# Later transposes of second-half token blocks, and a larger constant tile, in a fused decoder layer

## The chip, the cores and the metric

The kernel runs on one core of one Trainium2 chip. The metric is the device time of one execution in microseconds, the median of several runs. One launch computes the whole layer.

## The reference, cut to what matters

The layer prepends 16 meta tokens to 1024 tokens of width 1024, mixes them with two groups of heads, projects the mix with `w_out`, adds it to the residual stream and runs a gated feed-forward layer with a short convolution:

```python
h = concatenate([meta, x])                       # 1040 tokens
a = rmsnorm(h, ln_mix_pre)
proj = a @ w_in                                  # 1024 -> 3584
y_diff = diff_attention(dq, dk, dv, ...)         # 4 heads
y_hgrn = hgrn2(hq, hf, hi, hg, ...)              # 4 heads
mix = concatenate([y_diff, y_hgrn]) @ w_out      # 1024 -> 1024
h = h + rmsnorm(mix, ln_mix_post)
a = rmsnorm(h, ln_ffn_pre)
u = causal_conv3(a @ w_ffn_up) + conv_b          # 1024 -> 5632
y = (gelu(u[:, :2816]) * u[:, 2816:]) @ w_ffn_down
h = h + rmsnorm(y, ln_ffn_post)
return h[16:]
```

All inputs and outputs are float32.

## The kernel before, in words

Every large product is made of three products of float32r halves: an operand is split into a rounded part `hi` and a remainder `lo`, and `hi*hi`, `hi*lo` and `lo*hi` are added up in PSUM. The stages run one after the other: input projections together with attention and the recurrent heads; the output projection `w_out` in two column halves; the up-projection of the feed-forward layer, which uses a seven-product scheme on quarters of the matrices (names `pa`, `pb`, `pc`, in `unit`); and the down-projection (names `pd`), made of seven products as well.

**The stage around the change** is the second column half of the output projection (the loop `for i in range(1, NBLK)` that begins with `py = ps_b(f"py1_{i}")`). It runs over eight blocks of 128 tokens. Block i loads its mixed tokens into a tile `mp` (`second_load`, two transfers on the SP queue), and multiplies eight slices of 128 with the split weights, three matmuls of 512 columns each: `run(..., range(4), ...)` is the first twelve matmuls, `run(..., range(4, 8), ...)` the other twelve. Then `post(i, py)` does the norms: ScalarE squares `py` (`junk`), VectorE builds the new residual `xh`, ScalarE squares that, and VectorE writes the normed row block `a2` (printed as `a<-xh,ssy,gfb`). SP stores `xh` to DRAM (`hsc<-xh`).

`trans(i)` turns the normed block: eight 128x128 transposes on TensorE (`pa<-ident,a`, line 1230) into two PSUM banks, and ScalarE copies of them (`at<-pa`) into the tiles `at2` of two token halves: half 0 holds the tokens of blocks 0 to 4 and two of block 5, half 1 the rest. `trans(0)` is the short block of two meta rows. `t_split` and `t_sums` make the operands of the up-projection from `at2` on ScalarE (`t<-at`) and VectorE (`t<-at,t`, `at<-at`). The first up-projection matmuls (`pq`, in `plain_unit`) follow the loop, with `trans(7)` and `trans(8)` between them.

**Order.** TensorE's order is the order of the program (`manual_schedule` for that engine alone). The orders of VectorE, ScalarE, GpSimd and of the SP transfers are set when the kernel is built, by when each instruction is ready there. Each engine and each queue executes in order. Block i's tile `mp` is one of three places, shared in turn:

```python
SLOTS = (("X1", "X2", "mp", "X1", "X2", "mp", "X1", "X2"), ("mp", "X1", "X2", "mp", "X1", "X2", "X1", "mp"))
```

The second row is this stage: block 7 takes the place of block 5, block 6 that of block 3, block 8 that of block 4. Tokens `xh` and the row blocks `a2` have two places each, for odd and even blocks.

**Memory.** `const` tiles are the first on the left side of SBUF. The tiles of the pools opened on the left side follow them: among them the projection inputs `ahi` and `alo`, the blocks `X0`, `X1`, `X2` and `mp`, the split weights of `w_out` (`woh`, `wol`), and most of the up-projection's moving operands `t`. The weights of the projections, of the up-projection (`uh`, `ul`) and all matmul operands of the down-projection (`gh`, `gl`, `wh`, `wl`) are in pools on the right side, as are two of the fourteen operand tiles `t`.

Of the kernel before, what the change touches and what calls it, by code (L numbers as in the profile page):

```python
# [10 lines left out]
F32R = mybir.dt.float32r  # L11
# [6 lines left out]
P = 128  # L18
# [67 lines left out]
def layer_kernel(ctx: ExitStack, tc: tile.TileContext, x, meta, table, lbl, gpre, gpost, win,  # L86
# [25 lines left out]
    def const(shape, name, dt=F32):  # L112
        return cp.tile(shape, dt, tag=name, name=name)
# [12 lines left out]
    nlam = const([P, 1], "nlam")  # L126
    cwt = const([P, 2 * NF, 3], "cwt")
    cbt = const([P, 2 * NF], "cbt")
    m0 = const([P, 46], "m0", F32R)
    G.memset(m0.bitcast(F32), 0.0)  # L130
    m0_7 = const([P, 2, 1, 2], "m0_7", F32R)

# [850 lines left out]
    def load_wo(n):  # L983
        res = []
        for k in range(KD):
            raw = wp.tile([P, 512], F32, tag="wr", name=f"wor{n}_{k}", bufs=3)
            last_load.append(SY.dma_start(raw, wout[P * k: P * (k + 1), 512 * n: 512 * (n + 1)]))
            if n == 0 and k < 2:
                hi = wp.tile([P, 512], F32R, tag="wh", name=f"woh{n}_{k}", bufs=4)
                lo = wp.tile([P, 512], F32R, tag="wl", name=f"wol{n}_{k}", bufs=4)  # L990
            elif k < 5 if n == 0 else k > 5:
                hi, lo = (wsp.tile([P, 512], F32R, tag="wd", name=f"wo{x}{n}_{k}") for x in "hl")
            else:
                hi = wop.tile([P, 512], F32R, tag="woh", name=f"woh{n}_{k}")
                lo = wop.tile([P, 512], F32R, tag="wol", name=f"wol{n}_{k}")
            if n == 0:
                split(hi, lo, raw, V if k else G)
            else:
                with tc.issue_after(ends["a"].ins), tc.issue_after(ends["v"].ins):
                    split(hi, lo, raw, V if k % 2 else G, halved[0])  # L1000
            res.append((hi, lo))
        return res

    def tok(i):
        return (2, 14) if i == 0 else (P, start(i))

    def out_part(m, py, wo, ks, first, last):
        r = m.shape[-1]
        for k in ks:
            hi, lo = wo[k]  # L1010
            mh, ml = m[:, 0, k], m[:, 1, k]
            T.matmul(py[:r], mh, hi, start=(first and k == ks[0]), stop=False)  # L1012
            yield 216
            T.matmul(py[:r], mh, lo, start=False, stop=False)
            yield 216
            T.matmul(py[:r], ml, hi, start=False, stop=(last and k == ks[-1]))
            yield 216
    def meta_part(py, wo, full):
        for k in range(KD - 1):
            hi, lo = wo[k]  # L1020
            both = [(34, hi), (2, lo)]
            if k == KD - 2:
                both.reverse()
            for i, (r, w) in enumerate(both):
                T.matmul(py[:r], m0[:, 2 * k:2 * k + r], w, start=(k == 0 and i == 0), stop=(r == 34 and k == KD - 2))
                yield 216
            if k == 0 and full:
                yield from out_part(m0_7, py, wo[KD - 1:], range(1), False, False)
# [19 lines left out]
    def second_load(i):  # L1048
        blocks[i] = block_tile(1, i)
        block_load(blocks[i], i, 0, 4)  # L1050
        block_load(blocks[i], i, 4, 7 if i == 1 else 8)

    blocks = {}
# [6 lines left out]
    def y0_gain(p):  # L1060
        r = tok(p)[0]
        return G.tensor_tensor(y0[:r, p], y0[:r, p], gpo0[:r], op=ALU.mult)

    def out_last(p):
        r = tok(p)[0]
        py = ps_b(f"pz{p}")
        m = m0_7 if p == 0 else k7(p)
        for _ in out_part(m, py, wo0[KD - 1:], range(1), True, True):
            pass
        V.tensor_tensor(y0[:r, p], y0[:r, p], py[:r], op=ALU.add)  # L1070
        junk = qp.tile([P, 512], F32, tag="junk", name=f"jz{p}", bufs=1)
        A.activation(junk[:r], y0[:r, p], AF.Square, accum_out=ssy[:r, p, 0:1])
        A.activation(ssy[:r, p, 0:1], ssy[:r, p, 0:1], AF.Identity, bias=eps[:r], scale=1.0 / D)
        if p < 3:
            y0_gain(p)
# [27 lines left out]
    def ps_b(name):  # L1103
        return pp.tile([P, 512], F32, tag="b", name=name)
# [65 lines left out]
    wo = load_wo(1)  # L1170
# [11 lines left out]
    def load_xh(i):  # L1182
        r = tok(i)[0]
        if i:
            xhs[i] = qp.tile([P, D], F32, tag="xh", name=f"xh{i}")
        else:
            both = ep.tile([P, 2 * D], F32, tag="e0", name="xh0")
            xhs[i], xhs["sum"] = both[:, :D], both[:, D:]
        SY.dma_start(xhs[i][:r], meta[14:16, :] if i == 0 else x[P * (i - 1): P * i, :])
# [32 lines left out]
    def trans(i):  # L1222
        r, t0 = tok(i)
        a2 = a2t.pop(i)
        cs = slice(t0 - 14, t0 - 14 + r)
        for half in range(2):
            pt = ps_b(f"pa2_{i}_{half}")
            for j in range(4):
                k = 4 * half + j
                T.transpose(pt[:, j * r:(j + 1) * r], a2[:r, P * k: P * (k + 1)], ident[:r, :r])  # L1230
            pv = pt[:, : 4 * r].rearrange("p (k t) -> p k t", k=4)
            ks = slice(4 * half, 4 * half + 4)
            for p in range(2):
                lo_, hi_ = max(cs.start, C0[p]), min(cs.stop, C0[p] + 2 * WN[p])
                if lo_ < hi_:
                    A.copy(
                        at2[p][:, ks, lo_ - C0[p]:hi_ - C0[p]], pv[:, :, lo_ - cs.start:hi_ - cs.start])
# [10 lines left out]
    def t_split(p, j, src, where, *tag):  # L1248
        hi, lo = t_tiles(p, j, where, tag)
        A.copy(hi, src)  # L1250
        V.tensor_tensor(lo, src, hi.bitcast(F32), op=ALU.subtract)
        tt[p][j] = (hi, lo)

    def quarter(p, j):
        n = WN[p]
        a, c = {0: (0, 0), 7: (0, n), 4: (4, 0), 6: (4, n)}[j]
        return at2[p][:, a:a + 4, c:c + n]
# [12 lines left out]
    def run(*args):  # L1270
        for _ in out_part(*args):
            pass

    def k7(i):
        return m7[:, i - 1:i].rearrange("p b l t -> p l b t")

    for i in range(1, NBLK):
        py = ps_b(f"py1_{i}")
        if i >= 3:
            y0_gain(i)  # L1280
        if i == 1:
            load_xh(1)
            load_xh(0)
        if i + 1 < NBLK:
            second_load(i + 1)
            load_xh(i + 1)
        run(blocks[i], py, wo, range(4), True, False)
        if i == 3:
            trans(1)
        if i > 3:  # L1290
            trans(i - 2)
        if i == 5:
            trans(0)
        run(blocks[i], py, wo, range(4, 7 if i == 1 else 8), False, i > 1)
        if i == 1:
            pm = ps_b("py1_0")
            for _ in meta_part(pm, wo, True):
                pass
            for p in range(3):
                out_last(p)  # L1300
            run(k7(1), py, wo[KD - 1:], range(1), False, True)
            post(1, py)
            ysum = xhs.pop("sum")
            for l in range(2):
                A.copy(ysum[:2, 512 * l:512 * l + 512], pm[32 * l:32 * l + 2])
            G.tensor_tensor(ysum[:2, :512], ysum[:2, :512], ysum[:2, 512:], op=ALU.add)
            for p in (3, 4):
                out_last(p)
            continue
        post(i, py)  # L1310
        if i == 2:
            post(0, ysum[:, :512], ysum[:, 512:])
        if i == 5:
            t_split(0, 0, quarter(0, 0), ep, "e0")
            t_split(0, 4, quarter(0, 4), ep, "e1")
        if i == 7:
            t_split(0, 7, quarter(0, 7), mxp, "X2", WN[0])
            t_split(0, 6, quarter(0, 6), mxp, "X1", WN[0])
        if i in (2, 3):
            for p in (1 + 2 * i, 2 + 2 * i):  # L1320
                out_last(p)
# [366 lines left out]
```

## Time and profile before

| | |
|---|---|
| median of 3 runs | 1314.85 us (1314.73 to 1316.66) |
| the profiled execution | 1315.74 us |
| its span, first to last instruction | 1313.9 us |
| granted TensorE clock, mean | 0.996 |
| DVE (VectorE) busy | 887.4 us |
| ACT (ScalarE) busy | 697.6 us |
| POOL (GpSimd) busy | 482.0 us |

All times within the profile are microseconds from the start of the span. In a timeline row the first number is the start, the second the duration, then engine, line, operation, tiles and shape, the count of merged instructions, and in brackets the idle time before it with what ended it. Matmul rows overlap: a matmul is printed with its way through the array, and the next begins before it ends, so the distance from start to start is its cost.

### The profile page before, as it was taken

To read this page: it belongs to the slowest core of one execution; us is meant where nothing else is said; L and a number is where in the kernel's file an instruction comes from. 1 tells how busy PE (TensorE), PEld (TensorE's weight loads), DVE (VectorE), ACT (ScalarE), POOL (GpSimd) and SP (SyncE) were. 2 spreads that over 40 slices of the span, in tenths; PEclk is the share of its full clock that TensorE was granted. 3 is DMA by queue.
4 is the path that set the end of the run, shared out by engine and by line. 5 is a ranking of instruction groups with operands and counts; after the bars stand their busy time and mean duration, and the time that the engine had idled before them with its cause. 6 is when DMAs were issued, how large, how long until landed. Compare 5 with 4: busy or idle time off the path is not lost.

```text
span 1313.9 us, 26100 instructions
## 1 busy us (share of the span) xinstructions
PE 1283.4 (98%) x10154; PEld 1188.1 (90%) x10154; DVE 887.4 (68%) x1488; ACT 697.6 (53%) x1639; POOL 482.0 (37%) x387
## 2 busy tenths in 40 slices
PE   8999999999999999999999999999999999999997
PEld 7999999899989998777999999999999997888875
DVE  7574646465645574547897877877778768697586
ACT  8565466547644763456754544444544445464553
POOL 5231423232313310353066566576666631010121
PEclk9999999999999999998999999999999999999999
DMA  6243655273643533687222222222222138854263
GB/s 212 93 102 84 126 113 113 66 149 84 115 120 67 121 109 108 227 274 252 87 73 78 85 75 79 86 76 81 76 79 88 57 104 282 310 194 162 87 209 120
DMA packets 116418, 165.04 MB, mean 126 GB/s; under 512 B 10099, under 2 KB 57523, under 8 KB 116294
## 3 DMA queue, kind: packets, MB, share of 16 engines
q1 hardware_dynamic: 93062, 151.84, 34.9%
q0 software_dynamic: 23232, 11.54, 7.5%
q8 instruction: 80, 1.31, 0.4%
q14 instruction: 44, 0.36, 0.1%
HBM read 134.24 MB, written 52.17 MB: 142 GB/s over the span
## 4 chain that ended last, share of the span: by engine, by line
PE 49%; DVE 4%; ACT 2%; issue 1%; DVEq 0%; ACTq 0%
PE pd L1537 5%; PE pd L1538 5%; PE pd L1536 5%; PE pb L1378 4%; PE pb L1380 4%; PE pb L1379 4%; PE pa L1378 3%; PE pa L1380 3%; PE pa L1379 3%; PE pc L1380 3%; PE pc L1378 3%; PE pc L1379 3%; DVE t L53 1%; DVE c L53 1%; PE py L1012 1%
## 5 line engine op out<-in xcount | busy, mean ns | idle before, releaser
L1378 PE MATMUL pb<-t,uh 128*128 128x258 f32 x504 | 142.4, 283 | 2.3 <-DVE u L53 2.3
L1379 PE MATMUL pb<-t,uh 128*128 128x258 f32 x504 | 141.8, 281 | 0.0
L1380 PE MATMUL pb<-t,ul 128*128 128x258 f32 x504 | 141.8, 281 | 0.0
L1537 PE MATMUL pd<-wl,gh 128*128 128x512 f32 x308 | 122.0, 396 | 1.2 <-DVE wl L53 1.1
L1536 PE MATMUL pd<-wh,gh 128*128 128x512 f32 x308 | 121.7, 395 | 0.0
L1538 PE MATMUL pd<-wh,gl 128*128 128x512 f32 x308 | 121.6, 395 | 0.0
L53 DVE SCALAR_TENSOR_TENSOR c<-uu,cwt,c 128x514 f32<-128x514 f32 (+1 forms) x88 | 96.9, 1101 | 20.0 <-ACT c L53 19.3
L53 POOL TENSOR_TENSOR c<-c,c 128x514 f32<-128x514 f32 (+1 forms) x44 | 63.8, 1450 | 122.5 <-ACT c L53 119.1
L1378 PEld LDWEIGHTS pb<-t,uh 128*128 128x128 f32 x504 | 95.0, 189 | 2.7 <-DVE u L53 2.7
L1380 PEld LDWEIGHTS pb<-t,ul 128*128 128x128 f32 x504 | 95.1, 189 | 0.0
L1378 PE MATMUL pa<-t,uh 128*128 128x258 f32 (+1 forms) x336 | 95.1, 283 | 0.0
L1379 PEld LDWEIGHTS pb<-t,uh 128*128 128x128 f32 x504 | 95.1, 189 | 0.0
L1380 PE MATMUL pc<-t,ul 128*128 128x258 f32 (+1 forms) x336 | 95.0, 283 | 0.0
L1380 PE MATMUL pa<-t,ul 128*128 128x258 f32 (+1 forms) x336 | 94.9, 282 | 0.0
L1378 PE MATMUL pc<-t,uh 128*128 128x258 f32 (+1 forms) x336 | 94.7, 282 | 0.0
L1379 PE MATMUL pa<-t,uh 128*128 128x258 f32 (+1 forms) x336 | 94.6, 282 | 0.0
L1379 PE MATMUL pc<-t,uh 128*128 128x258 f32 (+1 forms) x336 | 94.5, 281 | 0.0
L53 DVE SCALAR_TENSOR_TENSOR c<-ug,cwt,c 128x514 f32<-128x514 f32 (+1 forms) x88 | 88.3, 1005 | 1.3 <-ACT c L53 0.6
L53 ACT CAST uh<-ra 128x512 fp32r<-128x512 f32 x67 | 41.2, 618 | 62.9 <-PE pb L1379 41.4
L53 POOL TENSOR_TENSOR ul<-ws,uh 128x512 fp32r<-128x512 f32 x42 | 59.1, 1408 | 39.3 <-ACT uh L53 39.3
L1537 PEld LDWEIGHTS pd<-wl,gh 128*128 128x128 f32 x308 | 57.7, 187 | 16.6 <-DVE wl L53 2.6
L53 DVE TENSOR_TENSOR ul<-ra,uh 128x512 fp32r<-128x512 f32 x42 | 39.8, 947 | 48.5 <-ACT uh L53 48.5
(388 smaller groups left out, 4176.3 us busy)
## 6 DMA issues: line engine op xcount, KB each, us to landing
ra<-in_wup_dram SPq DMA_DIRECT2D x88, 256.0 KB, 2.7
mp<-msc SPq DMA_DIRECT2D x23, 512.0 KB, 5.5
tsc<-in_wdown_dram SPq DMA_DIRECT2D x44, 256.0 KB, 4.4
wi<-tsc SPq DMA_DIRECT2D x44, 256.0 KB, 2.8
gi<-gsc SPq DMA_DIRECT2D x33, 256.0 KB, 4.7
wi<-in_wdown_dram SPq DMA_DIRECT2D x33, 256.0 KB, 5.2
gsc<-c SPq DMA_DIRECT2D x22, 257.0 KB, 2.1
tsc<-in_wdown_dram POOLq DMA_DIRECT2D x22, 256.0 KB, 7.4
```

Of the source, the lines that this page charges most:

```text
L53: ins = call(*args, **kw)
L1012: T.matmul(py[:r], mh, hi, start=(first and k == ks[0]), stop=False)
L1378: T.matmul(pt, hi[:, s], th[:, k], start=(first and k == 0), stop=False, skip_group_check=True)
L1379: T.matmul(pt, hi[:, s], tl[:, k], start=False, stop=False, skip_group_check=True)
L1380: T.matmul(pt, lo[:, s], th[:, k], start=False, stop=(k == 3), skip_group_check=True)
L1536: T.matmul(py, gh[:, s], wh, start=(k == 0 and pr not in (3, 7)), stop=False, skip_group_check=True)
L1537: T.matmul(py, gh[:, s], wl, start=False, stop=False, skip_group_check=True)
L1538: T.matmul(py, gl[:, s], wh, start=False, stop=(k == NH - 1), skip_group_check=True)
```

## The change

Two edits. In the loop above, the transposes of block i - 2 are issued behind all 24 matmuls of block i, for i from 4 to 8, where they stood between the first and the last twelve; the short `trans(0)` in pass 5 moves with them. `trans(1)` in pass 3 stays. And the constant tile `m0` is made 152 floats wide per partition, of which 46 are used as before.

```diff
-    m0 = const([P, 46], "m0", F32R)
+    m0 = const([P, 152], "m0", F32R)[:, :46]
     G.memset(m0.bitcast(F32), 0.0)
...
         run(blocks[i], py, wo, range(4), True, False)
         if i == 3:
             trans(1)
+        run(blocks[i], py, wo, range(4, 7 if i == 1 else 8), False, i > 1)
         if i > 3:
             trans(i - 2)
         if i == 5:
             trans(0)
-        run(blocks[i], py, wo, range(4, 7 if i == 1 else 8), False, i > 1)
         if i == 1:
```

## The prediction

> **What bounds the kernel now.** I read the page first (busy shares), then TensorE's own waits, then the timeline and the windows around the loop that is edited.
>
> ```profile
> PE 1283.4 (98%) x10154; PEld 1188.1 (90%) x10154; DVE 887.4 (68%) x1488; ACT 697.6 (53%) x1639; POOL 482.0 (37%) x387
> ```
> ```profile
> PE pa L1230 <- DVE a L53: 3.3, 1, 3.3
> ...
> PE pb L1378 <- DVE u L53: 2.3, 2, 1.4
> ```
>
> TensorE is busy for all but 30 us, so time can come from three things only: its waits, its clock, and what one matmul takes. Its longest single wait is the one that the first edit touches: transposes (line 1230) that wait 3.3 us for a normed row block. The timeline shows it in pass 5 of the loop, between the first and the last twelve matmuls of block 5:
>
> ```profile
> 607.07 0.40 PE L1016 MATMUL py<-woh,mp 128*128 128x512 f32 x1
> 610.73 1.97 PE L1230 MATMUL pa<-ident,a 128*128 128x128 f32 x8 [3.26 <-DVE a L53]
> 612.63 1.01 PE L1230 MATMUL pa<-ident,xh 2*128 2x2 f32 x8
> 613.57 0.80 PE L1012 MATMUL py<-woh,mp 128*128 128x512 f32 x1
> 614.16 0.63 PE L1014 MATMUL py<-wol,mp 128*128 128x512 f32 x1
> ...
> 617.51 0.39 PE L1016 MATMUL py<-woh,mp 128*128 128x512 f32 x1
> 617.75 0.39 PE L1012 MATMUL py<-woh,mp 128*128 128x512 f32 x1
> ...
> 620.53 1.03 PE L1230 MATMUL pa<-ident,a 128*128 128x128 f32 x8
> 621.32 0.48 PE L1012 MATMUL py<-woh,mp 128*128 128x512 f32 x1
> ...
> 624.38 0.47 PE L1012 MATMUL py<-woh,mp 128*128 128x512 f32 x1
> ```
> ```profile
> 600.00:610.00 10.00, 7.47 (x37) 5.78 (x35) 7.87 (x9) 7.17 (x25) 4.35 (x3) 0.98 0.59 201
> 610.00:620.00 10.00, 9.27 (x38) 7.71 (x39) 7.50 (x10) 5.98 (x16) 0.00 (x0) 0.68 0.74 232
> 620.00:630.00 10.00, 9.98 (x52) 8.01 (x52) 5.45 (x8) 6.62 (x19) 0.00 (x0) 1.00 0.59 177
> ```
>
> The wait costs twice. After it the granted clock is 0.68 (column behind POOL) for the next ten microseconds, eight transposes take 1.97 us where later ones take 1.03, and matmuls come every 0.43 us (614.16 to 614.59 and on) where later ones come every 0.23.
>
> **First edit, step by step.** A matmul of 512 columns costs 0.233 us at full clock (617.51 to 617.75 is one step), eight transposes 0.79 us (620.53 to 621.32). The two-row transposes take 0.94 us at the low clock (612.63 to 613.57), so I take 0.5 at full clock. Before, from the last matmul of block 5's first half (next slot free at 607.30) to the first matmul of block 6 (617.75) pass 10.45 us. That stretch holds 12 matmuls, eight transposes and eight short ones: 2.80 + 0.79 + 0.5 = 4.1 us of work, so 6.35 us are lost.
>
> After, the 12 matmuls run at once, to 610.10. Then the transposes still want the row block, which VectorE finishes here:
>
> ```profile
> 608.75 1.93 DVE L53 SCALAR_TENSOR_TENSOR a<-xh,ssy,gfb 128x1024 f32<-128x1024 f32 x1 [1.70 <-ACT ssy L53]
> ```
>
> 608.75 + 1.93 = 610.68, so a wait of 0.6 us stays. Behind it on TensorE stands block 6, and nobody waits for block 6 that early. It is too short for the clock to fall: the wait of 1.40 us quoted below leaves its window at 1.00. The transposes end at 610.73 + 0.79 + 0.5 = 612.0, and block 6 starts there instead of at 617.75. **TensorE gains 5.7 us.** No instruction is added or removed, and no transfer is in what moves.
>
> Of the later passes each transpose set moves 2.8 us back against its own block and so meets no wait: transposes of block 4 wanted a row block that is ready at 616.34 (row below) and now come at 617.6. The price is on the other side: the ScalarE copies and VectorE sums that read the transposes start only 5.9 - 2.8 = 3.1 us earlier in passes 7 and 8 instead of 5.9. VectorE is what ends the next waits of TensorE:
>
> ```profile
> 615.06 1.28 DVE L53 SCALAR_TENSOR_TENSOR a<-xh,ssy,gfb 128x1024 f32<-128x1024 f32 x1 [2.46 <-ACT ssy L53]
> ...
> 623.88 1.29 DVE L53 SCALAR_TENSOR_TENSOR a<-xh,ssy,gfb 128x1024 f32<-128x1024 f32 x1 [3.19 <-ACT ssy L53]
> ...
> 628.42 1.24 DVE L53 TENSOR_TENSOR at<-at 128x1032 f32<-128x1032 f32 x1 [1.27 <-ACT at L53]
> ...
> 643.47 1.28 DVE L53 SCALAR_TENSOR_TENSOR a<-xh,ssy,gfb 128x1024 f32<-128x1024 f32 x1 [1.45 <-ACT ssy L53]
> ```
> ```profile
> 671.84 0.39 PE L1378 MATMUL pb<-t,uh 128*128 128x258 f32 x1 [0.91 <-DVE u L53]
> ...
> 679.23 0.39 PE L1378 MATMUL pb<-t,uh 128*128 128x258 f32 x1 [1.40 <-DVE u L53]
> ```
> ```profile
> 670.00:680.00 10.00, 7.69 (x62) 7.28 (x62) 9.93 (x13) 3.86 (x8) 8.16 (x6) 1.00 0.23 80
> ```
>
> In 670 to 680 VectorE is busy 9.93 of 10 us and TensorE waits for it. So the 5.7 us arrive at the up-projection only as far as VectorE's own stream moves forward. Its idle time in the rows above is 2.46 + 3.19 + 1.27 + 1.45 = 8.4 us, so there is room. What releases it is half of it norm work, which moves with the matmuls (5.9 us earlier), and half transposes (3.1 us). The bounds are therefore 3.1 and 5.9. Neither kind is clearly the last, and I take the middle, **4.5 us**; the remaining 1.2 to 1.4 us would show as longer waits at the two `pb` rows.
>
> **Second edit.** 46 floats are 184 bytes, 152 are 608: everything behind it on the left side moves by 416 bytes a partition (the pools give each tile a multiple of 32: 192 become 608). It adds no instruction (the memset still covers 46 columns). What can change is what a matmul takes when its moving operand starts at another byte. The trace does have such a price:
>
> ```profile
> L1378 PE MATMUL pb<-t,uh 128*128 128x258 f32 x252 | 71.8, 285 | 2.3 <-DVE u L53 2.3
> L1380 PE MATMUL pb<-t,ul 128*128 128x258 f32 x252 | 71.2, 283 | 0.0
> L1379 PE MATMUL pb<-t,uh 128*128 128x258 f32 x252 | 71.1, 282 | 0.0
> L1379 PE MATMUL pb<-t,uh 128*128 128x256 f32 x252 | 70.7, 281 | 0.0
> L1378 PE MATMUL pb<-t,uh 128*128 128x256 f32 x252 | 70.6, 280 | 0.0
> L1380 PE MATMUL pb<-t,ul 128*128 128x256 f32 x252 | 70.5, 280 | 0.0
> ```
> ```profile
> 700.00:800.00 100.00, 100.00 (x839) 1.00 0.23 80
> ...
> 1140.00:1240.00 100.00, 100.00 (x431) 1.00 0.49 160
> ```
>
> The windows give the price of a column: in the up-projection 839 matmuls touch the 100 us, 2.3 of them only at the edges, so one takes 119.5 ns for 257 columns on average. In the down-projection (431, less 1.7) it is 232.9 ns for 512, 0.455 ns a column. At that rate 257 columns are 116.9 ns, so each of the 3528 matmuls of the up-projection (504 x 3 + 336 x 6, from the page) pays 2.6 ns above it, 9.2 us in all. That is the most that other bytes could give back. The other end: a 258-column operand's slices start in steps of 1032 bytes, a 256-column one's in steps of 1024, and the rows read 283.3 against 280.3 ns. Two columns are 0.9, so 2.1 ns are the price of starts at other bytes; if the 1764 matmuls of 256 columns paid it too, 3.7 us. Between -9.2 and +3.7 no row tells which byte is good: half of these matmuls already start at mixed bytes. I take **0**, as the row of 258 columns is the nearest and for it the move replaces one mix by another.
>
> [...]
>
> **The sum.** 1313.9 - 4.5 + 0 = 1309.4 us of span. Around the span of the profiled execution lie 1.84 us (1315.74 - 1313.9); it stands 0.89 above the median of the runs, so against that median: 1314.85 - 4.5 = **1310.3 us**.
>
> **Rivals.**
>
> A. *Block 7's load takes the wait's place.* It shares a place with block 5 and is issued here:
>
> ```profile
> 616.42 0.33 SPq L1189 DMA_DIRECT2D xh<-in_x_dram  x1
> 617.94 1.19 SPq L1041 DMA_DIRECT2D mp<-msc  x2
> ```
>
> The load of 617.94 waits for block 5's last matmul, and block 7 starts 6.4 us later (624.38). That matmul now ends near 610.3, but the queue is in order, and ahead stands the `xh` load, held until the row block of 616.34. If that order stays, the load goes out at 616.8, block 7 can start at 623.2, and TensorE, there at 618.4, waits 4.8 us and falls to the low clock again, which cost 10.45 - 4.1 - 3.4 = 2.9 us before. Gain 1.2, loss 2.9: 1.7 us slower, 1316.6. Against it: SP's order is set anew at the build by readiness, and the load would be ready 6 us before the other. 12 in 100. [...]
>
> B. *VectorE gives little.* Only the transposes' 3.1 us arrive and scheduling takes another microsecond: 2 us, 1312.8. 13 in 100.
>
> C. *The bytes make the up-projection slower.* From 4.5 us / 3528 = 1.3 ns a matmul on, the kernel is slower than before. If the 256-column half reached 285 ns and the other half as well, the worst of the six rows, it is (285 - 280.3 - 0.9) x 1764 + (285 - 283.3) x 1764 = 9.7 us, 1320.0 in all. Against: no operand shows that as its mean over all three lines. 9 in 100.
>
> D. *The bytes give back.* Half of the 9.2: 1310.3 - 4.6 = 1305.7. For: the excess is there to be had. Against: two rows are no sign that it depends on this one offset. 21 in 100.
>
> E. *The first edit does nothing*, since the row block comes later by what TensorE comes later: VectorE's 608.75 hangs on ScalarE (`ssy`), not on TensorE. 2 in 100, 1314.9.
>
> **How the numbers follow.** The forecast keeps 43 in 100; its own range, from 5.9 to 3.1 us of gain, is 1309.0 to 1311.8. D carries the range down to 1304.0. Up it goes to 1316.0, over B and E and to the edge of A; part of A, most of C and the deep end of D are left out, some 20 in 100. This kernel can be told from no change from about 0.2% on, 2.6 us, that is below 1312.2 or above 1317.5. Faster: the forecast, D and a fifth of B less a little of the forecast's upper tail, plus the part of C that only eats some of the gain, 0.70. Same: A, most of B, E, some of C, 0.21. Slower: the rest of C and a part of A, 0.09.
>
> **What would show it.** The wait at line 1230 in pass 5 falls from 3.3 us to under 1, and the clock reads 1.00 in 610 to 620: if not, the first step is wrong. Block 7's first matmul near 618.4 with its load issued before 612: right; a wait for a transfer there is A. The first `pq` matmul about 6 us earlier than before, and the two `pb` waits together 1 to 3 us longer. The up-projection's windows at 839 matmuls in 100 us: more is D, fewer is C. The prediction is wrong if the time is above 1312, or if the count of matmuls in those windows moves by more than 8.

## The result and the profile after

The changed kernel takes 1307.64 us (median of 6 runs, 1306.78 to 1309.35), the kernel before 1313.92 us beside it (6 runs, 1312.31 to 1316.66). The ratio is 0.9953, interval 0.9940 to 0.9967: 6.2 us less, 4.3 to 7.9. The profiled execution of after has 1307.29 us, its span 1305.5.

TensorE's waits in the stage (from 590 to 690 us: what waited, for what, us in all, times, longest), after:

```profile
PE pb L1378 <- DVE u L53: 2.5, 2, 1.4
PE py L1012 <- DMA mp<-msc: 1.3, 1, 1.3
PE pa L1230 <- DVE a L53: 0.7, 2, 0.4
```

The wait of 3.3 us at line 1230 has gone; two small ones, 0.7 us together, are left there. A new one, for block 7's load, stands at line 1012. The two `pb` waits are where they were (2.3 before). The timeline of TensorE around it, after:

```profile
607.40 0.40 PE L1016 MATMUL py<-woh,mp 128*128 128x512 f32 x1
607.88 1.09 PE L1230 MATMUL pa<-ident,a 128*128 128x128 f32 x8
608.91 0.66 PE L1230 MATMUL pa<-ident,xh 2*128 2x2 f32 x8
609.49 0.50 PE L1012 MATMUL py<-woh,mp 128*128 128x512 f32 x1
...
615.17 1.03 PE L1230 MATMUL pa<-ident,a 128*128 128x128 f32 x8
617.55 0.47 PE L1012 MATMUL py<-woh,mp 128*128 128x512 f32 x1 [1.34 <-DMA mp<-msc]
...
634.06 1.09 PE L1230 MATMUL pa<-ident,a 128*128 128x128 f32 x8 [0.45 <-DVE a L53]
```

Pass 5 now runs through: the last matmul of block 5, the transposes of this pass (blocks 3 and 0), and block 6 at 609.49. The eight transposes take 1.09 us where they took 1.97. SyncE's queue, after:

```profile
607.86 0.33 SPq L1189 DMA_DIRECT2D xh<-in_x_dram  x1
608.24 0.53 SPq L1041 DMA_DIRECT2D mp<-msc  x1
609.78 0.33 SPq L1210 DMA_DIRECT2D hsc<-xh  x1
610.20 1.85 SPq L1041 DMA_DIRECT2D mp<-msc  x2
616.21 0.33 SPq L1189 DMA_DIRECT2D xh<-in_x_dram  x1
```

Block 7's load (610.20) now stands ahead of the `xh` load that was before it. Block 5's last matmul ends at 607.80 (607.40 + 0.40), but the load goes out only 2.4 us later: ahead of it in the queue stands block 5's own store (`hsc<-xh`, 609.78), which waits until VectorE has finished `xh` at 609.75. Block 7 starts 7.4 us after the issue, 1.34 us later than TensorE could. The windows of after (busy time of PE, PEld, DVE, ACT, POOL, then granted clock, DMA share, GB/s):

```profile
600.00:610.00 10.00, 9.92 (x56) 7.98 (x55) 8.06 (x9) 5.55 (x19) 2.66 (x2) 1.00 0.61 205
610.00:620.00 10.00, 8.66 (x42) 6.94 (x42) 6.83 (x8) 8.36 (x23) 0.00 (x0) 1.00 0.91 313
620.00:630.00 10.00, 10.00 (x50) 8.17 (x49) 7.72 (x10) 5.84 (x17) 0.00 (x0) 1.00 0.56 168
700.00:800.00 100.00, 100.00 (x845) 100.00 (x844) 76.00 (x111) 47.93 (x86) 63.76 (x46) 1.00 0.24 80
```

The clock is 1.00 in all four (0.68 before in 610 to 620), the DMA engines are 0.91 busy while block 7's load is under way, and the up-projection runs 845 matmuls in 100 us instead of 839.

**Where the 8.4 us between the two traces lie.** First starts of TensorE, read from the timelines (us): block 4 and 6 of the second column half (line 1012), units 1 and 2 of the up-projection and its last matmul (lines 1378 to 1380), span end. A unit is 168 matmuls, 84 for each of the two token halves. Behind the bar stand differences between these times.

```
                      block 4  block 6  block 7   unit 1   unit 2     last  span end | 4->6   4->7   4->u1  4->u2  u2->last
before                 598.02   617.75   624.38   662.17   685.11  1086.63  1313.88  | 19.73  26.37  64.15  87.09  401.53
after                  595.56   609.49   617.55   655.94   678.92  1077.69  1305.51  | 13.93  21.99  60.38  83.36  398.78
before_again           598.62   618.43   624.98   662.77   685.71  1087.28  1314.49  | 19.81  26.36  64.15  87.09  401.57
move_only              599.94   613.59   621.66   659.53   682.46  1084.03  1311.67  | 13.64  21.72  59.59  82.52  401.57
bytes_only             596.39   614.75   621.18   658.86   681.83  1080.76  1308.21  | 18.36  24.80  62.47  85.44  398.93
move_256               596.45   610.78   618.71   656.73   679.67  1081.21  1308.42  | 14.33  22.26  60.28  83.22  401.55
swap_7_8               595.62   610.10   616.60   655.86   681.69  1080.27  1307.49  | 14.48  20.98  60.25  86.07  398.58
move_pass_5            595.96   610.63   618.47   656.18   679.37  1078.11  1305.46  | 14.67  22.51  60.22  83.41  398.74
half_pass_5            597.62   613.00   619.37   658.42   681.37  1080.16  1307.98  | 15.38  21.75  60.80  83.75  398.79
quarter_pass_5         594.61   613.96   620.34   658.08   681.07  1079.82  1307.04  | 19.35  25.72  63.46  86.45  398.76
bytes_160              595.27   609.89   617.83   656.60   679.69  1077.23  1304.59  | 14.62  22.55  61.33  84.42  397.54
vector_less            595.99   610.49   617.82   656.37   678.27  1077.02  1304.26  | 14.50  21.83  60.37  82.27  398.75
pass_5_and_bytes_160   595.58   609.49   617.55   655.17   678.26  1075.75  1303.00  | 13.90  21.96  59.59  82.68  397.49
pool_takes_one         595.60   610.22   618.26   655.87   679.83  1077.39  1304.68  | 14.62  22.66  60.27  84.23  397.57
```

From before to after: 2.46 us ahead of block 4, 3.73 from block 4 to unit 2, 2.75 from unit 2 to the last matmul of the up-projection, and 0.57 given back behind it: 8.37 in all. The runs say 6.2.

### The profile page after: what moved, and what is told of

It is laid out like the page before. It is cut to its first block, busy times and chain, and to the rows that moved or that the text cites. A ratio compares the mean times of both kernels' runs of the same rounds, so it can differ in the third digit from the quotient of the medians.

```text
span 1305.5 us, 26100 instructions
## 1 busy us (share of the span) xinstructions
PE 1277.2 (98%) x10154; PEld 1182.0 (91%) x10154; DVE 884.8 (68%) x1488; ACT 696.5 (53%) x1639; POOL 482.9 (37%) x387
## 4 chain that ended last, share of the span: by engine, by line
PE 81%; DVE 6%; DMA 4%; ACT 4%; issue 2%; SPq 0%; POOL 0%; DVEq 0%; ACTq 0%; POOLq 0%
PE pd L1537 5%; PE pd L1536 5%; PE pd L1538 5%; PE pb L1378 4%; PE pb L1380 4%; PE pb L1379 4%; PE pa L1378 3%; PE pa L1380 3%; PE pa L1379 3%; PE pc L1378 3%; PE pc L1379 3%; PE pc L1380 3%; PE pa L732 3%; PE pi_hf L234 1%; DMA ra<-in_wup_dram 1%
## 5 line engine op out<-in xcount | busy, mean ns | idle before, releaser
L53 POOL TENSOR_TENSOR c<-c,c 128x514 f32<-128x514 f32 (+1 forms) x44 | 63.8, 1449 | 122.4 <-ACT c L53 120.4
```

Of the source, the lines that this page charges most:

```text
L53: ins = call(*args, **kw)
```

## The experiments

The times of the runs are compared with the kernel before on the same chip. The expectations speak of a stretch that begins at "the first w_out matmul of the second half", at 510.36 us in before. That name is wrong: this matmul is the first of the first column half, some 88 us ahead of block 4, and what lies between has stops of its own. The results below are therefore read by the table's columns, from block 4 on.

**before_again.** No edit: a second trace of the kernel before.

> The kernel before, once more, for a second trace of it. Between the first two traces 3.0 us had already gone before the edited loop (first w_out matmul of the second half at 510.36 and 507.26 us), 1.2 us of it at a stop at 393.8 us (line 460, ended by 'issue') and 0.7 us at 482.3 us (line 651). Theory 1 (those two stops belong to one execution, not to the kernel): this trace lacks the stop at 393 and its loop begins near 508.3 to 509.5. Theory 2 (they belong to the kernel and the other bytes end them): the stops are there again and the loop begins near 510.4. Both: up-projection windows of 839 matmuls per 100 us, wait of 3.3 us at line 1230 in pass 5.

Measured: 1.0012 (1.0002 to 1.0021) against itself, so that a tenth of a per cent means nothing here. From block 4 to unit 2 and from there to the last matmul it repeats before to 0.04 us. The stop at 393 us was there again (0.9 us), with a further one at 272 us (0.7), so theory 1 missed. But such stops, ended by nothing that the trace shows ("issue"), come in other kernels too, with either size of `m0`: none to 1.7 us at 272, none to 1.3 us at 393. All three traces with `m0` at 46 floats have the one at 393, of the eleven others only move_pass_5 has it in full. Whether the bytes have a part in it stays open.

**move_only.**

```diff
 # after, with
-    m0 = const([P, 152], "m0", F32R)[:, :46]
+    m0 = const([P, 46], "m0", F32R)
```

> The transposes' move alone, m0 at 46 floats. Theory 1 (the two edits add up; the move gives what the loop shows, the bytes what the up-projection and the projections show): 3.0 to 3.6 us below before, near 1310.5; from the first w_out matmul of the second half to the first matmul of the up-projection's unit 1 148.7 us as in the trace of after (151.8 before); up-projection unchanged from before (424.5 us from its first to its last matmul). Rival (the move gives all of it and the bytes nothing): 6.3 us below before, 1307.6. Rival (the bytes give all, the loop's gain is taken back later): no change, 1313.9.

**bytes_only.**

```diff
 # before, with
-    m0 = const([P, 46], "m0", F32R)
+    m0 = const([P, 152], "m0", F32R)[:, :46]
```

> The larger m0 alone, the loop as before. Theory 1: 2.7 us less in the up-projection (421.8 us instead of 424.5 from its first to its last matmul), 0.5 to 1.5 us less in the input projections, 2.7 to 4.0 us below before in all, 1310 to 1311; the wait of 3.3 us at line 1230 is there. Rival (the move gives all): no change, 1313.9, the up-projection 424.5 us.

Measured: the move alone 0.9976 (0.9967 to 0.9985), 3.2 us less; the bytes alone 0.9979 (0.9965 to 0.9992), 2.8 us less. Their sum of 6.0 is close to the 6.2 of both together. The traces part them. In the up-projection, windows of move_only:

```profile
700.00:800.00 100.00, 100.00 (x839) 100.00 (x839) 77.27 (x110) 47.00 (x84) 63.27 (x45) 1.00 0.24 80
```

and of bytes_only:

```profile
700.00:800.00 100.00, 100.00 (x845) 100.00 (x845) 75.99 (x110) 47.76 (x85) 63.84 (x45) 1.00 0.25 83
```

From unit 2 on the move gives nothing (401.57 us) and the bytes give 2.6 (398.93). From block 4 to unit 2 the three traces with twelve and twelve matmuls in pass 5 take 87.09, 87.09 and 85.44 us, the three with all moved 83.36, 82.52 and 83.22: 3.5 us on average (3.2 with a fourth of this order, bytes_160 below, at 84.42). 3.5 and 2.75 are 6.25, near the runs' 6.2. So what the first pair of traces shows ahead of block 4 hardly counts in the medians.

**move_256.**

```diff
 # after, with
-    m0 = const([P, 152], "m0", F32R)[:, :46]
+    m0 = const([P, 112], "m0", F32R)[:, :46]
```

> Both edits, but m0 at 112 floats: the later tiles move by 256 bytes instead of 416, so that each starts at the same byte of a 256-byte unit as before. Theory 1a (what counts is the place within 128 or 256 bytes): up-projection as before, 424.5 us, whole time that of the move alone, about 1310.5. Rival 1b (any move of the bytes, or larger units, decide): up-projection differs from 424.5 by more than 0.5 us. [...]

Measured: 0.9979 (0.9970 to 0.9988), the ratio of the move alone. The windows of move_256:

```profile
700.00:800.00 100.00, 100.00 (x839) 100.00 (x838) 76.35 (x109) 47.81 (x85) 62.40 (x45) 1.00 0.24 80
```

839 again, and 401.55 us from unit 2 on. Theory 1a holds: a move by 256 bytes gives the old time (401.53 in before, 401.57 in move_only), one by 416 does not (398.78 in after). If the place within one unit decides, these times say that the unit divides 256 and, as 416 is 13 times 32, is larger than 32 bytes.

**bytes_160.**

```diff
 # after, with
-    m0 = const([P, 152], "m0", F32R)[:, :46]
+    m0 = const([P, 72], "m0", F32R)[:, :46]
...
     t2_cm, t2p = pool("tsplit2", 1)
+    t2p.tile([P, 16], F32, tag="pad", name="pad")
```

> As after in the loop, but the bytes chosen by the traces: m0 at 72 floats and an unused tile of 64 bytes ahead of the last three operands, so that the six 256-column operands that lie alone on the left side (j = 0, 1, 2, 3, 4, 5 of the second half) all start 32 bytes behind a multiple of 128. In after three of them do (j = 1, 2, 3: 117.9, 113.3 and 114.0 ns a matmul) and three start at 96 (j = 0, 4, 5: 120.0, 119.2, 119.9). Theory (the place within 128 bytes sets the duration): those three fall to 113 to 118 ns, the up-projection from its first to its last matmul takes 418.5 to 420.5 us (421.8 in after), the time 1.5 to 3 us below after. Rival (the place matters only together with the neighbours, one choice is as good as another): 421 to 424.5 us, time as after or up to 2.7 us slower.

Measured: 0.9947 (0.9931 to 0.9963). From unit 2 on 397.54 us, 1.2 less than after, and 420.63 from unit 1: just outside what the theory expected, better than the rival. The time is 0.8 us below after by the two ratios, less than expected and within the intervals. The windows of bytes_160:

```profile
700.00:800.00 100.00, 100.00 (x849) 99.85 (x847) 76.78 (x111) 47.98 (x86) 63.96 (x46) 1.00 0.23 80
```

What one matmul of 256 columns takes from start to start (middle 80% of 252 each), by operand, with the operand's first byte behind a multiple of 128. The traces hold no addresses; the bytes are those at which the built programs place the tiles (`m0` at 5728 in all three, the tile behind its 184 bytes at 5920 in before):

```
second token half, operand j:   0          1          2          3          4          5
before      byte, ns          64 119.4    0 117.8    0 116.9    0 116.9   64 120.3   64 119.8
after                         96 120.0   32 117.8   32 113.3   32 114.0   96 119.2   96 119.9
bytes_160                     32 117.9   32 117.9   32 113.3   32 114.3   32 113.7   32 113.8
```

The operands brought from byte 96 to byte 32 fell from 119.2 and 119.9 to 113.7 and 113.8, and from 120.0 to 117.9. So the place decides, but not alone: at one place some operands take 113 to 114 ns and others 118. What parts those is open. Against after, this edit moves operands 0, 4 and 5 by 320 bytes, five times 64, so a unit that decides is larger than 64 bytes; the runs do not part 128 from 256.

The table leaves out why so little of this arrives. 13.7 ns off for 12 matmuls in 20 units would be 3.3 us, and 1.2 came. Operand 5 of the first token half went from 118.4 to 122.4 ns, about 1 us. And every second unit loses 0.12 to 0.23 us around its first matmul with operand 3, so that units take 19.80 us and 19.92 to 20.03 in turn, where nearly all of after's take 19.93. What is waited for there is not shown.

**half_pass_5 and quarter_pass_5** give a part of the wait back.

```diff
 # after; half: 6 and range(6, 8), quarter: 5 and range(5, 8)
-        run(blocks[i], py, wo, range(4, 7 if i == 1 else 8), False, i > 1)
+        run(blocks[i], py, wo, range(4, 6 if i == 5 else 7 if i == 1 else 8), False, i > 1 and i != 5)
         if i > 3:
             trans(i - 2)
         if i == 5:
             trans(0)
+            run(blocks[i], py, wo, range(6, 8), False, True)
```

> As after, but in pass 5 the transposes stand behind 18 of the 24 matmuls, so that half of the wait at line 1230 comes back (3.3 us less six matmuls, 1.4: about 1.5 to 1.9 us), and half of it only. Theory (a wait of this size leaves the clock up, as the waits of 1.2 to 1.4 us do): clock 1.00 in the ten microseconds behind it, block 6 starts 1.5 to 1.9 us later against the matmuls before it, most of which block 7's load would have cost anyway: stretch 148.5 to 149.5 us. Rival (any wait over about 1.4 us brings the low clock, as those of 2.8 to 3.3 us do): clock near 0.7 behind it, 3 us more, stretch 151 to 152, nothing left of the move.

> As half_pass_5, but pass 5's transposes stand behind 15 of the 24 matmuls, so that about 2.1 us of the wait at line 1230 come back (1.43 us with 18 of 24, clock 1.00 behind it; 2.8 to 3.3 us with 12 of 24, clock 0.5 to 0.7 for some 4 us behind it). If 2.1 us still leave the clock up: stretch to unit 1 148.0 to 149.2 us, clock 1.00 in every five microseconds. If they do not: clock 0.6 to 0.9 in one or two of them, stretch 150 to 152, as with 12 of 24.

The wait and two windows behind it, half_pass_5:

```profile
609.90 1.09 PE L1230 MATMUL pa<-ident,a 128*128 128x128 f32 x8 [1.43 <-DVE a L53]
```
```profile
610.00:615.00 5.00, 5.00 (x31) 4.20 (x32) 3.05 (x4) 3.14 (x9) 0.00 (x0) 1.00 0.84 265
615.00:620.00 5.00, 5.00 (x28) 4.15 (x27) 4.30 (x5) 2.56 (x7) 0.00 (x0) 1.00 0.63 204
```

and quarter_pass_5:

```profile
607.39 1.97 PE L1230 MATMUL pa<-ident,a 128*128 128x128 f32 x8 [2.62 <-DVE a L53]
```
```profile
605.00:610.00 5.00, 2.61 (x15) 2.29 (x16) 3.85 (x4) 3.01 (x10) 1.25 (x1) 0.68 0.70 220
610.00:615.00 5.00, 5.00 (x17) 4.05 (x17) 3.29 (x3) 4.70 (x13) 0.00 (x0) 0.64 0.59 224
```

In these two traces a wait of 1.43 us leaves the clock at 1.00; one of 2.62 (2.1 was expected) does not. The first costs next to nothing in the end: block 6 starts 1.45 us later against block 4 than in after (15.38, 13.93), but the first half of block 7's load is in by then (0.4 us of waiting is left, for the second half), and unit 2 is reached in 83.75 us, after's 83.36. The second reaches it in 86.45. So 1.2 us more wait cost 2.7 us, and the low clock is the other thing that the windows show to have changed.

The times do not part the two: 0.9962 (0.9948 to 0.9976) and 0.9961 (0.9945 to 0.9977). The mean clock of every execution is on record, and it says that neither trace stands for all executions of its kernel. In the traces this mean is 0.995 or 0.996 with 6.8 us of low clock in the stage, 0.996 or 0.997 with 3.4 us, and 0.997 or 0.998 with none. Of the seven executions of half_pass_5 three have 0.995, so the clock does not stay up each time (at which wait it falls the mean does not say), and of the five of quarter_pass_5 one has 0.998. All 40 executions of after, move_only, move_256, move_pass_5 and bytes_160, where the wait is gone, have 0.997 or 0.998 (vector_less and pass_5_and_bytes_160, where it is gone as well, have one of 0.996 in four and in six). The kernel before shows the price: of its 73 executions beside the experiments 42 have 0.995 or less and take 1315.4 us on average, and 13 have 0.997 or more and take 1312.4; the second group is the faster on each of the four chips, by 1.4 to 4.8 us. These 3.0 us at one and the same program are nearly the 3.2 that the move gave. That it is the clock that makes most of the gain is well supported by this, though no run sets the clock by itself.

**move_pass_5.**

```diff
 # after, with
+        if i > 5 or i == 4:
+            trans(i - 2)
         run(blocks[i], py, wo, range(4, 7 if i == 1 else 8), False, i > 1)
-        if i > 3:
-            trans(i - 2)
         if i == 5:
+            trans(3)
             trans(0)
```

> As after, but only pass 5's transposes (blocks 3 and 0) stand behind the last twelve matmuls; passes 4, 6, 7 and 8 have them in the middle again. Theory (all of the gain is pass 5's wait and the clock behind it, the other four moves give nothing): wait at line 1230 in pass 5 under 0.5 us, clock 1.00, the stretch from the first w_out matmul to unit 1 at 147.5 to 149.0 us, time within 1 us of after. Rival 1 (the later transposes want row blocks that are not ready in the middle of passes 6 and 7): waits at line 1230 of 0.5 us or more in passes 6 or 7, in all 1 to 3 us, stretch 149.5 to 151. Rival 2 (moving the later ones back was a loss, as they feed VectorE 2.8 us later): stretch below 147.5.

Measured: 0.9953 (0.9939 to 0.9967), the same as after. From block 4 to unit 2 83.41 us, after 83.36: the four other moves give and cost nothing. (The expectations' own stretch is 146.6 us, which by its letter is rival 2; what is short in it lies ahead of block 4.)

**swap_7_8** takes the new wait away.

```diff
 # after, with
-    SLOTS = (..., ("mp", "X1", "X2", "mp", "X1", "X2", "X1", "mp"))
+    SLOTS = (..., ("mp", "X1", "X2", "mp", "X1", "X2", "mp", "X1"))
...
         if i == 7:
             t_split(0, 7, quarter(0, 7), mxp, "X2", WN[0])
+        if i == 8:
             t_split(0, 6, quarter(0, 6), mxp, "X1", WN[0])
```

> As after, but block 7 takes the place of block 4 and block 8 that of block 5, so that block 7's load can go out a block earlier; the split of quarter 6, which takes that place next, moves behind block 8. Measured from the first w_out matmul of the second half to the first matmul of unit 1 (151.8 and 152.5 us in two traces of before, 148.7 in after, 147.9 with the move alone). Theory (what is left of the wait is block 7's load): the wait of 1.2 to 1.4 us at line 1012 is gone and the stretch is 146.6 to 147.6 us, the time 0.8 to 1.3 us below after. Rival (VectorE's own stream sets when the up-projection can begin): the wait at line 1012 is gone, but 0.8 to 1.3 us appear at line 1230, at pq or at pb, the stretch is 147.8 to 148.7 and the time as after.

TensorE's waits of swap_7_8 from 590 to 690 us:

```profile
PE pb L1379 <- DVE u L53: 3.9, 1, 3.9
PE pa L1230 <- DVE a L53: 1.9, 2, 1.3
```

Measured: 0.9974 (0.9963 to 0.9984), slower than after by 2.8 us, with intervals that just touch. The load's wait is gone and block 7 starts 1.0 us sooner (20.98, 21.99), but at the transposes of block 7 TensorE waits 1.3 us (0.45 in after), and unit 1 is reached as in after (60.25, 60.38): VectorE ends block 7's row block at 633.9 us here and at 634.0 in after. Here the rival is right. Behind it 2.7 us are lost at `pb`: one wait of 3.9 us stands in place of two that make 2.5, and the clock behind it is 0.66 from 675 to 680 us. That the wait is longer because the edit also moved a split, which gives VectorE another order, is argued and not shown.

**vector_less.**

```diff
 # after, in t_split
-        V.tensor_tensor(lo, src, hi.bitcast(F32), op=ALU.subtract)
+        if (p, j) in ((1, 3), (1, 5)):
+            A.copy(lo, src)
+        else:
+            V.tensor_tensor(lo, src, hi.bitcast(F32), op=ALU.subtract)
```

> As after, but the remainders of two up-projection operands (j = 3 and 5 of the second token half) are plain copies made by ScalarE instead of differences made by VectorE, so that these two operands' low parts are not the reference's; two VectorE instructions of 1.22 us fall out of its unbroken run from 639 to 674 us, and nothing falls out on TensorE. Theory (VectorE's stream ends the last waits of the stage, so what TensorE gains ahead of it is given back there): the two pb waits, 2.5 us in after, fall to 0.2 to 1.0 us, unit 1 takes 21.0 to 22.0 us instead of 22.97, the time is 1 to 2.3 us below after. Rival (the pb waits hang on something else, such as the up-projection's weights or ScalarE, which gets the two copies): 2 to 3.5 us of waits stay and the time is that of after or up to 1 us above.

This kernel leaves out the differences of two operands, so its results are not the reference's. TensorE's waits from 590 to 690 us:

```profile
PE pb L1381 <- DVE u L53: 1.7, 1, 1.7
PE pa L1230 <- DVE a L53: 1.2, 2, 0.6
PE py L1012 <- DMA mp<-msc: 0.6, 1, 0.6
```

Measured: 0.9940 (0.9927 to 0.9953). One of the two `pb` waits is gone, the other is 1.7 us; unit 1 takes 21.90 us (678.27 - 656.37) instead of 22.98. Two instructions of 1.22 us less on VectorE brought 1.1 us: it does end these waits, but less of them than was expected.

**pass_5_and_bytes_160** is `move_pass_5` with the two lines of `bytes_160`.

> The two versions that did best put together: only pass 5's transposes moved, and the bytes of the run before (m0 at 72 floats, 64 unused bytes ahead of the last three operands). Theory (the effects add up): stretch to unit 1 as with pass 5 alone (146.6 us, unit 1 23.2), up-projection from unit 2 on 397.5 us as with these bytes (398.8 in after), time 1.5 to 2.5 us below after, 1305.0 to 1306.1. Rival (what pass 5 alone gained in the stretch belongs to that one trace, or the bytes change the waits): stretch 147.7 to 148.7, time 1306.2 to 1307.6.

Measured: 1305.25 us, 0.9935 (0.9921 to 0.9949). 82.68 us from block 4 to unit 2, 397.49 from there: from unit 2 on the bytes give the same as alone, with either order of the transposes. It has the lowest time of the study, 8.5 us below before. That it is below after as well (0.9953, interval to 0.9940) rests on the 1.3 us from unit 2 on; the intervals overlap, and the 0.7 us ahead of unit 2 lie within what single traces of one order differ by (82.52 to 84.42).

**pool_takes_one.**

```diff
 # pass_5_and_bytes_160, in t_split
-        V.tensor_tensor(lo, src, hi.bitcast(F32), op=ALU.subtract)
+        (G if (p, j) == (0, 5) else V).tensor_tensor(lo, src, hi.bitcast(F32), op=ALU.subtract)
```

> As pass_5_and_bytes_160, but the remainder of one operand (j = 5 of the first token half, 1032 columns) is made by GpSimd, which is idle from 606 to 655 us, in place of VectorE, whose run is unbroken from 639 to 674 us. Theory (VectorE's stream ends the two pb waits; with two such instructions gone they fell from 2.5 to 1.7 us and unit 1 from 22.97 to 21.90 us): unit 1 falls from 23.1 to 22.2 to 22.9 us, the time by 0.2 to 0.9 us, to 1304.3 to 1305.0. Rival (GpSimd gets little of its turn while VectorE runs unbroken: one of its 512-column differences took 4.95 us at 655 us and 1.35 to 1.75 later; the weights' remainders queued behind this one come late): new waits of TensorE for POOL, unit 1 at 23.1 us or longer, time 1305.3 to 1309.

Measured: 0.9936 (0.9921 to 0.9952), no gain; unit 1 takes 23.96 us (679.83 - 655.87), 0.9 more. TensorE's wait at `pb`, from 590 to 690 us:

```profile
PE pb L1379 <- DVE u L53: 2.1, 1, 2.1
```

The timeline of GpSimd:

```profile
644.58 2.80 POOL L53 TENSOR_TENSOR t<-at,t 128x1032 fp32r<-128x1032 f32 x1 [37.10 <-ACT t L53]
```

and of VectorE:

```profile
645.30 3.17 DVE L53 TENSOR_TENSOR at<-at 128x1024 f32<-128x1024 f32 x1
648.39 2.35 DVE L53 TENSOR_TENSOR t<-at,t 128x1024 fp32r<-128x1024 f32 x2
650.66 1.21 DVE L53 TENSOR_TENSOR at<-at 128x1024 f32<-128x1024 f32 x1
```

While GpSimd works, VectorE's instruction of 1.21 us takes 3.17 and ends 1.1 us after GpSimd's, as if it had waited for it: the 1.2 us taken off VectorE were paid back with 0.8 more. The `pb` waits did fall, from 2.7 us in two to one of 2.13, but this one brought the low clock (0.71 from 665 to 670 us, 0.95 from 670 to 675), which the two shorter ones of pass_5_and_bytes_160 (1.23 and 1.46) did not. That is neither theory nor the rival as written (no wait for POOL appears). What held VectorE up there is not shown.

## Why the prediction was right, and where it was not

The time fell, by 6.2 us where 4.5 were forecast; 1307.6 lies in the range (1304.0 to 1316.0) but below the forecast's own (1309.0 to 1311.8): the range reaches there only because of rival D. Two terms were off, the second by more, and in opposite directions, so the sum is nearer than its larger miss.

**TensorE gains 5.7 us at block 6: right.** From block 4 to block 6 19.73 us became 13.93, 5.8 less; the move alone gives 6.1. The wait, the clock, and block 6 right behind the transposes came as worked out. The remaining wait was put at 0.6 us; it is under 0.1 in after, and 0 to 0.8 in the other traces of that order. The reading that the wait costs twice was right too, and half_pass_5, quarter_pass_5 and the record of the clock add that most of the loss that counts is the clock's.

**4.5 us arrive at the up-projection: right within its bounds (3.1 and 5.9), wrong in where the rest goes.** 3.7 us arrive in the pair of traces, 3.5 in the means. (The upper bound of 5.9 is a little more than the 5.7 of the step before it.) The prediction let 1.2 us be lost at the two `pb` rows; these went from 2.3 to 2.5 only. The step that failed is the load: "no transfer is in what moves", and with that no term for block 7's. Rival A set the load's 6.4 us against TensorE, but only for the case that it stays behind the `xh` load. For the new order the prediction took it to be in time, as it would have been if issued when block 5 ended (607.80 + 6.4 = 614.2, and TensorE came for it at 616.21). Instead block 5's store held it in the queue until 610.20 and it took 7.4 us, so block 7 waited 1.34, and from block 4 to block 7 the gain shrank from 5.8 to 4.4. The signs named for it, issue before 612 and block 7 near 618.4, came (610.20, 617.55) by luck: this trace is 2.46 us ahead at block 4 already. Counted from block 4, 618.4 is 20.4 us, and block 7 starts at 21.99. VectorE behind it takes its part all the same: where swap_7_8 removed the load's wait, the gain went at the transposes of block 7, not to the up-projection. So VectorE does bound what arrives, as argued, though by a wait ahead of unit 1. That the later sets pay for being moved back ("only 3.1 us earlier") did not show: move_pass_5 is as fast.

**The bytes give 0: wrong, and the larger miss.** They give 2.75 us, 0.8 ns for each of 3528 matmuls (845 - 2.3 in 100 us are 118.7 ns, against 119.5). The excess of 2.6 ns over the column rate was read correctly (119.5 ns against 116.9). The step that failed is the choice of 0 because "the move replaces one mix by another": the mixes are not alike, for all slices of a 256-column operand, 1024 bytes apart, have the same place within 128 bytes and fall together (operands 2 and 3 from 116.9 ns to 113.3 and 114.0). These operands, the second token half, give 1.75 of the 2.75 us; the other 1.0 come from the 258-column operands of the first half, whose slices do lie at mixed places, and that part has no explanation here. Three operands at byte 0 took 117 to 118 ns, at byte 32 113 to 118; those at 64 and 96 took 119 to 120 either way.

**The rivals.** D was in part the case: 2.75 of its 4.6 us. A came as a shadow: SP's order was set anew, as held against it, and what is left is 1.3 us of waiting for the transfer, without the low clock. B (2 us) fell to the 3.5 measured, C to the 845 matmuls, and E to move_only's 3.2 us. The signs named in advance came out so: wait and clock right; the first `pq` matmul 6.9 us earlier by the traces, of which 2.5 lie ahead of block 4, so by 4.4 instead of 6; the `pb` waits not longer; the count up by 6, towards D.

## What to carry to other kernels

A wait of an otherwise full TensorE is to be read with the clock behind it: from 1.4 to 2.6 us its price in two traces here rose from next to nothing (0.4) to 3.1 us against after. Filling half of it with work already at hand kept the clock up in four of seven executions (mean 0.997 or 0.998), filling all of it in the 40 counted above. When an engine is made earlier, set each load that its end releases against the new time of its first reader, with the load's own landing time (7.4 us here) and with what stands ahead of it in its queue (a store, 2.4 us here). A constant's size is a lever on the tiles behind it, 2.75 us in the up-projection here: where matmuls such as these, of 256 and 258 columns, fill a stage, look at their start-to-start times by the byte at which the operand begins before calling that neutral.

## What was not expected of the hardware

In these traces the low clock came in stretches of 3.41 us or of twice that, behind waits from 2.13 us up, and it did not always begin with the wait. In all fourteen, between 60 and 1290 us, each wait of TensorE from 2.13 us up (2.13, 2.62, 2.82, 2.87, 3.26, 3.89) has a stretch at half clock (0.50 granted) in it or up to 1.6 us behind it, and none up to 1.72 us has one. The stretch is 3.41 us long after three of them and 6.83, twice as long, after the other three. Waits of 2.62 and 3.26 us had it at once (eight transposes in 1.97 us). In bytes_only a wait of 2.87 us was followed by eight transposes at full speed, and the slow matmuls came 1.6 us after work had begun again:

```profile
608.70 1.09 PE L1230 MATMUL pa<-ident,a 128*128 128x128 f32 x8 [2.87 <-DVE a L53]
609.72 0.66 PE L1230 MATMUL pa<-ident,xh 2*128 2x2 f32 x8
610.31 0.80 PE L1012 MATMUL py<-woh,mp 128*128 128x512 f32 x1
611.75 0.63 PE L1012 MATMUL py<-woh,mp 128*128 128x512 f32 x1
```

So nearly the same wait cost a different amount in two executions: 19.8 us from block 4 to block 6 with 2.82 us and the longer stretch (before_again), 18.4 with 2.87 us and the shorter one (bytes_only). What sets the start and the length of a stretch is not shown.

The start-to-start times of the same matmul mostly repeat to the nanosecond from unit to unit (within 1 ns in 97% of cases in before), and over fourteen traces the up-projection from unit 2 on took 401.53 to 401.57, 398.58 to 398.93 or 397.49 to 397.57 us, by its bytes alone.
